# A hybrid attention and DeltaNet block: other cost figures in the planner that sets the engines' orders

## The chip, the cores and the metric

The kernel runs on one core of one Trainium2 chip. The metric is the device time of one execution in microseconds (us); a comparison uses the median over several executions. The core has five engines that work at once, each in the order of its own instruction list: TensorE (PE, with its weight loads PEld), VectorE (DVE), ScalarE (ACT), GpSimd (POOL) and SyncE (SP). DMA transfers are issued from SP, ACT and POOL. An engine whose next instruction waits for a semaphore holds back everything behind that instruction on the same engine.

## The reference, cut to what matters

One layer over 1024 tokens of 1024 channels. The normed input is projected to 7184 columns; two token mixers read them in parallel; gates merge their outputs; an output product, a residual and a final norm follow.

```
h    = rmsnorm(x, norm_w);  proj = h @ w_in
# mixer A: three dilated window attentions (dilation 1, 4, 16), rotary positions, 8 heads of 64
q, k = rope(q), rope(k)
o_g  = softmax(q k^T / 8, masked) v          # for g = 0, 1, 2
o_a  = sum_g softmax_g(lse_g) * o_g
# mixer B: gated DeltaNet, chunks of 64 tokens
q, k, v = silu(conv4(.));  q, k = l2norm(.)
T    = (I + strict(beta k k^T * decay))^-1   # triangular solve, per chunk and head
u, w = T (beta v), T (beta k exp(G))
scan over chunks: v_new = u - w S;  o = q_dec S + attn v_new;  S = S*dec + k_dec^T v_new
# both
y = sig(gate_a) * (o_a*silu(z_a)) @ w_up_a + sig(gate_b) * (rms(o_b)*silu(z_b)) @ w_up_b
out = rmsnorm(x + y @ w_out, final_norm_w)
```

## The kernel before, in words

**Products.** The projection goes in units of 256 columns. Operands are split into a high and a low float16 part, and every product is three matmuls (lines L184, L185, L186: high by high, low by high, high by low), most with a moving block of 512 columns. Some units, the four value blocks among them, go as seven products of sums of blocks (`seven_products`, L355) in place of eight; DVE adds those sums (L329) and ACT and DVE split them (L330). These seven products are the same in the kernel before and after. Weights come through two `wstage` buffers, loaded by POOL (the first ones by SP), and are split by ACT into `whi` (L167) and by DVE into `wlo` (L84 is the line of the helper that issues most DVE operations with three operands, L87 that of the ones with two).

**Stages.** The start (0 to about 45 us) loads x and the first weights, norms, and makes the first queries and keys (L444 to L480). Then come the three attentions, each in two halves of four heads (`att_run`, L758): scores (L790, L792), the masked maximum on DVE (L799, tile `sm`), the exponent on ACT (L803), transposes on PE (L813, into a bank `ps_G`), a split of the transposed weights (`th` on ACT, L818; `tl` on DVE) and the product with the values (L840, `Vh` and `Vl`). `combine` (L866) reads partial results `og` back by DMA and copies their statistics `md` (L873). Projection matmuls of later units are fed in between, so that PE has work while a softmax is under way. From about 440 us on come the DeltaNet's decay terms (L1080 to L1129; `softplus` needs an ACT table of its own, loaded at L1091, and the exponent's table is loaded again at L803), its short convolution (`conv_unit`, L993: tiles `xc` and `ca`), the pairs of keys, and for each half of the heads (`hb` = 0, 1) a triangular solve on DVE (`solve`, L1305: X in 31 pairs of steps, then X times `bsc`, then T1). The solve writes X and T1 to DRAM (`u_d`, `t_d`) and gathers them again with DMAs of 128-byte runs: four pieces into `MT` (L1335) and two pieces into `T1p` (L1333). `merge` (L1339) multiplies them with small matmuls (L1350 left, which reads `T1p`, and L1365 right, which reads `Y`). Then come the chunk states, the scan over chunks, the up-projection, the output product and the final norm.

**What sets the order.** PE's order is written out by hand. The orders of DVE, ACT, POOL and SP are made when the program is built, by a planner at the end of the file. `steps_of` (L2064) turns every instruction into a `Step` with the steps that must end before it (`deps`) or only be issued before it (`turn`). `Step.cost` (L2013) gives each a time for which it holds its engine (`hold`) and a time until its result is there (`ns`), from its shape:

```
kb = w[0].total / 1024
self.hold, self.ns, self.pass_ns = 330 + 0.25 * kb, 2000 + (2.2 if w[0].dram else 5.5) * kb, 60
if min(w[0].piece, r[0].piece) < 256:
    self.hold = 1400 if kb > 64 else 600
    self.ns = self.hold + 2500
if self.eng == "POOL":
    self.hold = 530
```

`fill` (L2132) plays the program through with these figures: whenever an engine is free, it takes of the steps whose inputs are there the one with the lowest rank. `set_orders` (L2196) makes a forward pass by written order, a backward pass that gives each step its latest start, another forward pass by these latest starts, and so on, and keeps the order of the pass that ended first (`PASSES = 2`). The order so found is fixed in the program. Stretches of the program inside `with in_order():` (L496, the start, and L1910, the end) keep their written order on DVE and ACT, DMAs left out.

Of the kernel before, what the change touches and what calls it, by code (L numbers as in the profile page):

```python
# [17 lines left out]
PSUM = bass.MemoryType.PSUM  # L18
# [60 lines left out]
def hybrid_block(ctx: ExitStack, tc: tile.TileContext, A):  # L79
# [415 lines left out]
    ss = base.tile([128, 8], F32, name="ss0")  # L495
    with in_order():  # L496
        wq, wk = w_first
# [1451 lines left out]
TABLE_NS = 1283  # L1949
TILE_SWITCH_NS = 150  # L1950
PASSES = 2


class Operand:


    def __init__(self, b, write):
        size = SIZES[b.dtype]
        ap = [tuple(x) for x in b.ap]
        self.name, self.size, self.write, self.dram = b.tensor.name, size, write, "DRam" in type(b.tensor).__name__  # L1960
        self.psum = b.tensor.name.startswith("ps_")
        if self.dram:
# [29 lines left out]
    def meets(self, o):  # L1992
        if not self.psum and not all(a[0] < b[1] and b[0] < a[1] for a, b in ((self.rows, o.rows), (self.bytes, o.bytes))):
            return False
        return self.dram or self.psum or (self.mask() & o.mask()) != 0


class Step:


    def __init__(self, i, ins):
        self.i, self.ins, self.kind = i, ins, type(ins).__name__
        self.deps, self.turn, self.succ = set(), set(), []
        self.table, self.small, self.hold, self.ns, self.pass_ns = 0, False, 0, 0, 35
        self.args = []
        self.eng = None
        if self.kind not in ("BassTilePoolBoundary", "InstTileManualSchedule"):
            self.eng = ENGINES[str(ins.engine).split(".")[-1]]
            self.args = [Operand(a.bass_ap, w) for l, w in ((ins.outs, True), (ins.ins, False)) for a in l
                         if getattr(a, "bass_ap", None) is not None]  # L2010
            self.cost()

    def cost(self):  # L2013
# [16 lines left out]
        elif self.kind == "InstDMACopy":  # L2030
            kb = w[0].total / 1024
            self.hold, self.ns, self.pass_ns = 330 + 0.25 * kb, 2000 + (2.2 if w[0].dram else 5.5) * kb, 60
            if min(w[0].piece, r[0].piece) < 256:
                self.hold = 1400 if kb > 64 else 600
                self.ns = self.hold + 2500
            if self.eng == "POOL":
                self.hold = 530
        elif self.eng == "DVE":
# [25 lines left out]
def steps_of(tc, in_order):  # L2064
    steps = [Step(i, ins) for i, ins in enumerate(tc.nc.cur_bb.bb.instructions)]
    written, read, users, place = {}, {}, {}, {}
    for s in steps:
        for x in s.args:
            for j, y in written.get(x.name, []) + (read.get(x.name, []) if x.write else []):
                if j not in s.deps and x.meets(y):  # L2070
                    s.deps.add(j)
        for x in s.args:
            (written if x.write else read).setdefault(x.name, []).append((s.i, x))
            users.setdefault(x.name, set()).add(s.i)
        s.deps.discard(s.i)

    def behind(later, earlier):
        for i in later:
            steps[i].deps.update(j for j in earlier if j < i)

# [20 lines left out]
    for s in steps:  # L2101
        if s.kind != "BassTilePoolBoundary" or s.ins.bass_pool_name not in pools:
# [14 lines left out]
    for a, b in in_order:  # L2117
        last = {}
        for s in steps[a:b]:
            if s.eng in ("DVE", "ACT") and s.kind != "InstDMACopy":  # L2120
                if s.eng in last:
                    s.deps.add(last[s.eng])
                last[s.eng] = s.i
    for s in steps:
        s.deps = {j for j in s.deps if steps[j].eng}
        s.turn -= s.deps | {s.i}
        for j in s.deps | s.turn:
# [3 lines left out]

def fill(steps, rank, back):  # L2132
# [4 lines left out]
    free, due, open_ = {e: 0.0 for e in order}, {e: [] for e in order}, {e: [] for e in order}  # L2137
    pe = [s.i for s in steps if s.eng == "PE"][::-1 if back else 1]
    events, blocked, table, small = [(0.0, e) for e in order], set(), 0, None

    def known(i):
        if steps[i].eng not in (None, "PE"):
            heapq.heappush(due[steps[i].eng], (ready[i], i))

    for s in steps:
        if not left[s.i]:
            known(s.i)
    while events:
        t, e = heapq.heappop(events)
        if t < free[e]:  # L2150
            heapq.heappush(events, (free[e], e))
            continue
        if e == "PE":
            if len(order[e]) == len(pe):
                continue
            i = pe[len(order[e])]
            if left[i]:
# [5 lines left out]
        else:  # L2163
# [19 lines left out]
        for j in s.deps | s.turn if back else s.succ:  # L2183
            o = steps[j]
            ready[j] = max(ready[j], t + s.hold + o.until(s) - o.hold if back else t + extra + s.until(o))
            left[j] -= 1
            if not left[j]:
                known(j)
                if o.eng in blocked:
                    blocked.discard(o.eng)  # L2190
                    heapq.heappush(events, (max(free[o.eng], ready[j]), o.eng))
    assert sum(len(x) for x in order.values()) == sum(s.eng is not None for s in steps)
    return start, order, max(t + s.ns for s, t in zip(steps, start))


def set_orders(tc, in_order):  # L2196

    steps = steps_of(tc, in_order)
    rank = [float(s.i) for s in steps]
    best = None  # L2200
    for _ in range(PASSES):
        start, order, end = fill(steps, rank, False)
        if best is None or end < best[0]:
            best = end, order
        late = fill(steps, [-t for t in start], True)[0]
        rank = [-t - s.hold for s, t in zip(steps, late)]
    start, order, end = fill(steps, rank, False)
    if end < best[0]:
        best = end, order
    order_only = mybir.DependencyInfo(mybir.DependencyClass.NoSync, mybir.DependencyReason.DATA)  # L2210
    for e, ids in best[1].items():
# [3 lines left out]
    return best[0]  # L2215

# [105 lines left out]
```

## Time and profile before

| what | value |
|---|---|
| median of 3 executions | 1079.28 us (1072.13 to 1081.35) |
| the profiled execution | 1086.27 us |
| its span, first to last instruction | 1084.5 us |
| TensorE's mean granted clock in it | 0.990 |
| busy DVE in it | 879.6 us (81%) |
| busy ACT in it | 572.0 us (53%) |
| first matmul, and the end of the last | 5.18 us and about 1077 us |

A matmul's record is longer than the time for which it holds PE: matmuls are pipelined, so the pitch from one start to the next counts. A row of the timeline gives the start, the duration, the engine, the line, the operation with its tiles, and in brackets the idle time before it with what ended it. In a window's row the columns are the window's length, the busy time of PE, PEld, DVE, ACT and POOL, then PE's granted clock, the DMA share and GB/s.

### The profile page before, as it was taken

How to read it: one execution, taken by the hardware profiler on the slowest of the kernel's cores; microseconds unless marked ns; L12 is line 12 of the kernel's file. 1: busy time of each engine (PE TensorE's matmuls, PEld its weight loads, DVE VectorE, ACT ScalarE, POOL GpSimd, SP SyncE). 2: the span in 40 equal slices, each digit the busy share in tenths (PEclk: the TensorE clock that was granted, in tenths of full speed). 3: DMA queues.
4: the chain of work that ended last, by engine and by line, in shares of the span. 5: the costliest groups of instructions: out<-in, count | busy, mean ns of one | idle time of the engine just before them, and what ended most of it. 6: DMA issues, size and time to landing. Idle time of an engine off the chain costs nothing.

```text
span 1084.5 us, 24950 instructions
## 1 busy us (share of the span) xinstructions
PE 1047.0 (97%) x9986; PEld 639.9 (59%) x9986; DVE 879.6 (81%) x2030; ACT 572.0 (53%) x1306; POOL 56.1 (5%) x107
## 2 busy tenths in 40 slices
PE   6999999999989999989999999999899999999997
PEld 5995695865846855866655545545445555444444
DVE  6897988979959889989956797796288669799934
ACT  6445766766656666657645623244244336434523
POOL 0000000000000000000010000110200000000000
PEclk9999999999999999999999999999899999999999
DMA  7243532532623622551233466766675413743132
GB/s 259 77 137 97 138 107 85 139 93 84 177 70 103 166 90 75 145 159 45 65 133 106 122 167 185 253 200 207 203 257 175 154 60 129 289 156 117 59 117 78
DMA packets 99780, 148.53 MB, mean 137 GB/s; under 512 B 31168, under 2 KB 64704, under 8 KB 98512
## 3 DMA queue, kind: packets, MB, share of 16 engines
q1 hardware_dynamic: 69264, 84.64, 26.9%
q0 software_dynamic: 12320, 44.11, 12.8%
q10 hardware_dynamic: 18080, 18.20, 4.8%
q8 instruction: 78, 1.28, 0.5%
q14 instruction: 38, 0.31, 0.1%
HBM read 91.13 MB, written 36.90 MB: 118 GB/s over the span
## 4 chain that ended last, share of the span: by engine, by line
PE 41%; DVE 14%; issue 3%; DMA 3%; ACT 3%; POOL 0%; ACTq 0%; DVEq 0%; SPq 0%; POOLq 0%
PE ps_mm L184 10%; PE ps_mm L186 9%; PE ps_mm L185 9%; DVE ca L84 3%; PE ps_S L186 1%; PE ps_S L185 1%; PE ps_S L184 1%; DVE sm L799 1%; DVE tl L87 1%; DVE wlo L84 1%; PE ps_G L186 1%; PE ps_G L185 1%; PE ps_G L184 1%; DMA wn_d<-uw 1%; PE ps_S L1706 1%
## 5 line engine op out<-in xcount | busy, mean ns | idle before, releaser
L186 PE MATMUL ps_mm<-h_hi,wlo 128*128 128x512 f16 (+1 forms) x552 | 208.9, 378 | 0.0
L184 PE MATMUL ps_mm<-h_hi,whi 128*128 128x512 f16 (+1 forms) x492 | 186.6, 379 | 0.0
L185 PE MATMUL ps_mm<-h_lo,whi 128*128 128x512 f16 (+1 forms) x492 | 186.3, 379 | 0.0
L186 PEld LDWEIGHTS <-wlo 128*128 128x128 f16 x788 | 77.4, 98 | 87.2 <-issue 1.8
L185 PEld LDWEIGHTS <-whi 128*128 128x128 f16 x848 | 83.5, 98 | 72.7 <-issue 6.3
L184 PEld LDWEIGHTS <-whi 128*128 128x128 f16 x848 | 83.6, 99 | 69.3 <-issue 1.4
L803 ACT ACTIVATE sm<-sm,osb 128x128 f32<-128x128 f32 (+1 forms) x160 | 69.3, 434 | 63.4 <-DVE osb L799 62.5
L799 DVE CUSTOM_DVE_ANT_0 sm<-ps_S,amask 128x128 f32<-128x128 f32 (+1 forms) x192 | 59.4, 346 | 8.4 <-PE ps_S L792 8.4
L87 DVE TENSOR_TENSOR tl<-ps_G,th 128x256 f16<-128x256 f32 (+1 forms) x96 | 52.0, 542 | 17.3 <-ACT th L818 16.7
L84 DVE SCALAR_TENSOR_TENSOR wlo<-wstage,whi 128x1024 f16<-128x1024 f32 x42 | 51.1, 1220 | 17.5 <-ACT whi L167 15.7
L330 ACT ACTIVATE whi<-wstage 128x512 f16<-128x512 f32 x76 | 46.0, 626 | 32.0 <-DVE wstage L329 9.8
L185 PE MATMUL ps_mm<-wlo,h_hi 128*128 128x256 f16 (+1 forms) x256 | 57.3, 246 | 0.0
L84 DVE SCALAR_TENSOR_TENSOR whi<-wstage,whi 128x512 f16<-128x512 f32 x76 | 51.9, 686 | 6.6 <-ACT whi L330 6.2
L84 DVE SCALAR_TENSOR_TENSOR ca<-xc,cw,ca 128x512 f32<-128x512 f32 x72 | 53.8, 747 | 2.6 <-ACT ca L1010 2.1
L167 ACT ACTIVATE whi<-wstage 128x1024 f16<-128x1024 f32 x41 | 42.7, 1053 | 22.0 <-PE ps_mm L185 11.6
L813 PE MATMUL ps_G<-cons,sm 128*128 128x128 f32 x280 | 48.5, 278 | 5.2 <-ACT sm L803 4.5
L329 DVE TENSOR_TENSOR wstage<-wstage 128x512 f32<-128x512 f32 x76 | 52.1, 688 | 1.1
L813 PEld LDWEIGHTS ps_G<-cons,sm 128*128 128x128 f32 x280 | 35.0, 142 | 21.7 <-ACT sm L803 7.4
L818 ACT CAST th<-ps_G 128x256 f16<-128x256 f32 (+1 forms) x96 | 43.8, 456 | 5.3 <-PE ps_G L813 4.4
L184 PE MATMUL ps_mm<-whi,h_hi 128*128 128x256 f16 (+1 forms) x192 | 46.5, 256 | 0.0
L186 PE MATMUL ps_mm<-whi,h_lo 128*128 128x256 f16 (+1 forms) x192 | 46.2, 255 | 0.0
L184 PE MATMUL ps_mm<-h_hi,wlo 128*128 128x512 f16 x120 | 45.6, 380 | 0.0
(489 smaller groups left out, 2893.6 us busy)
## 6 DMA issues: line engine op xcount, KB each, us to landing
wstage<-in_w POOLq DMA_DIRECT2D x68, 512.0 KB, 4.6
og<-osb ACTq DMA_DIRECT2D x32, 132.0 KB, 2.2
og<-og SPq DMA_DIRECT2D x32, 132.0 KB, 2.3
gspb<-gst ACTq DMA_DIRECT2D x16, 256.0 KB, 4.2
sga<-gspa SPq DMA_DIRECT2D x8, 512.0 KB, 9.6
wstage<-in_w_up POOLq DMA_DIRECT2D x8, 512.0 KB, 4.4
sgb<-gspb SPq DMA_DIRECT2D x8, 512.0 KB, 4.0
wos<-in_w_out SPq DMA_DIRECT2D x8, 512.0 KB, 4.1
```

The costliest lines, as they stand in the source:

```text
L84: (eng or V).scalar_tensor_tensor(out, in0, scalar, in1, op0=op0, op1=op1)
L87: (eng or V).tensor_tensor(out, in0, in1, op)
L167: SC.activation(hi[:, 4 * c:4 * c + 4], st, AF.Copy, scale=W_SCALE)
L184: PE.matmul(out, lhsT=wh(k), rhs=mh(k), start=first and i == 0, stop=False, skip_group_check=True)
L185: PE.matmul(out, lhsT=wh(k), rhs=ml(k), start=False, stop=False, skip_group_check=True)
L186: PE.matmul(out, lhsT=wl(k), rhs=mh(k), start=False, stop=last and i == len(ks) - 1, skip_group_check=True)
L329: V.tensor_tensor(self.part[name], self.part[x], self.part[y], ALU.add)
L330: SC.activation(t[:, b, 0], self.part[name], AF.Copy, scale=W_SCALE)
L799: V.tensor_tensor_reduce(P[:, u, :128 * nk], psc[:, u * 256:u * 256 + 128 * nk], mask, -cexp, -NEG, ALU.add, ALU.min, accum_out=osb[:, 256 ...
L803: SC.activation(P[:, u, :128 * nk], P[:, u, :128 * nk], AF.Exp, bias=osb[:, 256 + hd:257 + hd], scale=-1.0, accum_out=osb[:, 260 + hd:261 ...
L813: PE.transpose(pt[:, c:c + 128], P[:, u, i * 128:i * 128 + 128], ident)
L818: SC.copy(th[:, :n], pt[:, :n])
```

## The change: what it does

The diff touches only the planner and one `in_order`. No instruction is added to the kernel, none is taken away, PE's order is the same row for row (14460 rows), and so is POOL's; what changes is in which order DVE, ACT and SP do the same work. Line numbers after L1950 shift.

- DMAs cost more in the plan: until landing 2800 ns + 4 or 7 ns a KB (before 2000 + 2.2 or 5.5), another 2800 ns where runs are under 256 bytes; issue 350 to 590 ns by the number of rows. A queue moves a KB in 4 ns, and a transfer that is behind others on its queue lands later.
- DVE and ACT operations cost 3% more, a change between small and large matmul tiles 300 ns (before 150). Both kernels make three forward and two backward passes; the constant counted the backward ones and now counts the forward ones.
- `in_order` fixes the order on every engine but PE, DMAs included, as an order of issue; and the first stretch now begins at the program's first instruction, so the first loads go in written order.
- Accesses to one DRAM tensor bind each other only where they meet byte for byte.

```diff
-    def in_order():
-        n = len(nc.cur_bb.bb.instructions)
+    def in_order(first=None):
+        n = len(nc.cur_bb.bb.instructions) if first is None else first
...
-    with in_order():
+    with in_order(0):
...
-TILE_SWITCH_NS = 150
-PASSES = 2
+TILE_SWITCH_NS = 300
+QUEUE_NS = 4
+PASSES = 3
...
-        return self.dram or self.psum or (self.mask() & o.mask()) != 0
+        return self.psum or (self.mask() & o.mask()) != 0
...
-            self.hold, self.ns, self.pass_ns = 330 + 0.25 * kb, 2000 + (2.2 if w[0].dram else 5.5) * kb, 60
+            rows = max(x.rows[1] - x.rows[0] for x in self.args)
+            self.hold = 590 if rows <= 32 else 500 if rows <= 64 else 350
+            self.ns, self.pass_ns, self.kb = 2800 + (4 if w[0].dram else 7) * kb, 60, kb
             if min(w[0].piece, r[0].piece) < 256:
                 self.hold = 1400 if kb > 64 else 600
-                self.ns = self.hold + 2500
+                self.ns += 2800
             if self.eng == "POOL":
-                self.hold = 530
+                self.hold = 530 if rows > 64 else 630
...
+        if self.eng in ("DVE", "ACT") and not self.kb:
+            self.hold, self.ns = 1.03 * self.hold, 1.03 * self.ns
...
-            if s.eng in ("DVE", "ACT") and s.kind != "InstDMACopy":
+            if s.eng not in (None, "PE"):
                 if s.eng in last:
-                    s.deps.add(last[s.eng])
+                    s.turn.add(last[s.eng])
...
-        start[i], free[e] = t, t + s.hold + extra
+        start[i], free[e] = t, t + s.hold + late
+        if s.kb and not back:
+            moved[e] = max(moved[e], t) + s.kb * QUEUE_NS
+            late = max(0, moved[e] + 1200 - t - s.ns)
```

How the rows move is shown at three places. The first is DVE in the attention of the second group, at about 298 us of the profile before; `md_5829` waits for the DMA of `og_5826`, `Vl_3943<-ps_mm_3945` is what frees a bank for PE, and `sm_4518` is the first softmax of the next half. Before:

```order
L84 SCALAR_TENSOR_TENSOR Vl_3943<-rx_4394,Vh_3942 128x4x128
L873 COPY md_5829<-og_5826 128x16
L84 SCALAR_TENSOR_TENSOR Vl_3943<-ps_mm_3945,Vh_3942 128x4x128
L84 SCALAR_TENSOR_TENSOR wlo_4481<-wstage_3966,wlo_4481 128x512
L799 ISA sm_4518,osb_4512<-ps_S_4513,amask_757 128x128
```

After:

```order
L84 SCALAR_TENSOR_TENSOR whi_4449<-wstage_3966,whi_4449 128x512
L84 SCALAR_TENSOR_TENSOR Vl_3943<-ps_mm_3945,Vh_3942 128x4x128
L84 SCALAR_TENSOR_TENSOR wlo_4481<-wstage_3966,wlo_4481 128x512
L873 COPY md_5829<-og_5826 128x16
L799 ISA sm_4518,osb_4512<-ps_S_4513,amask_757 128x128
```

The copy `md` went from ahead of that `Vl` to behind it and behind `wlo`, but stands ahead of `sm` still.

The second place is ACT at the decay terms, at about 477 us; `ba`, `bg` and `tmpa` are the decay terms' tiles, `xc_7352` and `ca_7355` belong to a convolution, `sm_7413` to the softmax for which PE's next transposes wait. Before:

```order
L1080 ACTIVATE ba_7193<-ps_O_7194 128x128
L1094 ACTIVATE ea_7375<-cons_78 128x8
L1085 ACTIVATE bg_7365<-ba_7193 128x64
L1090 ACTIVATE tmpa_7366<-tmpa_7366 128x64
L1091 ACT_TABLE_LOAD
L1091 ACTIVATE tmpa_7366<-tmpa_7366,onec_87 128x64
L1008 COPY xc_7352<-ps_mm_7327 128x512
L900 COPY osb_6503<-ps_G_7396 128x256
L1010 ACTIVATE ca_7355<-ps_mm_7327,cw_84 128x512
L901 DMA oa_d_733<-osb_6503 128x2x128
L803 ACT_TABLE_LOAD
L803 ACTIVATE sm_7413,osbs_7407<-sm_7413,osbs_7407 128x128 x2
```

After:

```order
L1080 ACTIVATE ba_7193<-ps_O_7194 128x128
L1094 ACTIVATE ea_7375<-cons_78 128x8
L1008 COPY xc_7352<-ps_mm_7327 128x512
L1010 ACTIVATE ca_7355<-ps_mm_7327,cw_84 128x512
L1085 ACTIVATE bg_7365<-ba_7193 128x64
L900 COPY osb_6503<-ps_G_7396 128x256
L1090 ACTIVATE tmpa_7366<-tmpa_7366 128x64
L901 DMA oa_d_733<-osb_6503 128x2x128
L1091 ACT_TABLE_LOAD
L1091 ACTIVATE tmpa_7366<-tmpa_7366,onec_87 128x64
L803 ACT_TABLE_LOAD
L803 ACTIVATE sm_7413,osbs_7407<-sm_7413,osbs_7407 128x128 x2
```

The two copies and `ca` went from between the two table loads to ahead of the first. On DVE, `ba` moved ahead of both `wlo` pieces there, and `sm_7413` ahead of eight rows of the decay terms.

The third place is SP behind the second solve (`hb` = 1), at about 721 us. Before:

```order
L1326 DMA u_d1_9510<-X_9411 128x1024
L1327 DMA t_d1_9511<-T1_9508 128x1024
L1335 DMA MT1_8544<-u_d1_9510 32x32x32
L1333 DMA T1p_9514<-t_d1_9511 32x32x32 x2
L1335 DMA MT1_8544<-u_d1_9510 32x32x32 x2
L1393 DMA kbt_10633<-kb_d1_8558 128x1024
L1335 DMA MT1_8544<-u_d1_9510 32x32x32
L1393 DMA kbt_10637<-kb_d1_8558 128x1024
```

After:

```order
L1326 DMA u_d1_9510<-X_9411 128x1024
L1327 DMA t_d1_9511<-T1_9508 128x1024
L1335 DMA MT1_8544<-u_d1_9510 32x32x32 x4
L1333 DMA T1p_9514<-t_d1_9511 32x32x32 x2
L1393 DMA kbt_10633<-kb_d1_8558 128x1024
L1393 DMA kbt_10637<-kb_d1_8558 128x1024
```

Both `T1p` pieces went behind all four `MT` pieces, and both `kbt` behind all six. On DVE, one `wlo` piece and one `ca` now stand ahead of X times `bsc` of this solve, and one more `ca` ahead of `T1_9508`. At the start, SP now issues `cons`, `amask` and the two key-weight pieces ahead of the fourth x tile and of the `xs` tiles, which stood ahead of them.

More of the change, by code (lines that the diff above doesn't have):

```diff
@@ L2077, in behind @@
     def behind(later, earlier):
-        for i in later:
-            steps[i].deps.update(j for j in earlier if j < i)
+        if later and earlier:
+            steps.append(Step(len(steps), None))
+            steps[-1].deps |= earlier
+            for i in later:
+                steps[i].deps.add(steps[-1].i)
     for t in tc.info.tiles:
@@ L2100, in steps_of @@
                 used[n] |= users.get(t.name, set())
-    for s in steps:
+    for s in list(steps):
         if s.kind != "BassTilePoolBoundary" or s.ins.bass_pool_name not in pools:
@@ L2136, in fill, with passed @@
     start, order = [0.0] * len(steps), {e: [] for e in ENGINES.values()}
-    free, due, open_ = {e: 0.0 for e in order}, {e: [] for e in order}, {e: [] for e in order}
-    pe = [s.i for s in steps if s.eng == "PE"][::-1 if back else 1]
-    events, blocked, table, small = [(0.0, e) for e in order], set(), 0, None
+    free, moved, due, open_ = [{e: x() for e in order} for x in (float, float, list, list)]
+    events, blocked, table, small, end = [(0.0, e) for e in order], set(), 0, None, 0.0
     def known(i):
[L2142 to L2147, printed above, removed]
+        e = steps[i].eng
+        if e is None:
+            passed(steps[i], ready[i], 0)
+        elif e not in given:
+            heapq.heappush(due[e], (ready[i], i))
+        if e in blocked:
+            blocked.discard(e)
+            heapq.heappush(events, (max(free[e], ready[i]), e))
+    def passed(s, t, late):
+        for j in s.deps | s.turn if back else s.succ:
+            o = steps[j]
+            if back:
+                ready[j] = max(ready[j], t + s.hold + o.until(s) - o.hold)
+            else:
+                ready[j] = max(ready[j], t + late * (s.i in o.deps) + s.until(o))
+            left[j] -= 1
+            if not left[j]:
+                known(j)
+    for i in [s.i for s in steps if not left[s.i]]:
+        known(i)
     while events:
@@ L2179, in fill, with orders_of @@
             small = s.small
-        start[i], free[e] = t, t + s.hold + extra
+        start[i], free[e] = t, t + s.hold + late
+        if s.kb and not back:
+            moved[e] = max(moved[e], t) + s.kb * QUEUE_NS
+            late = max(0, moved[e] + 1200 - t - s.ns)
+        end = max(end, t + late + s.ns)
         order[e].append(i)
         heapq.heappush(events, (free[e], e))
[L2183 to L2191, printed above, removed]
-    assert sum(len(x) for x in order.values()) == sum(s.eng is not None for s in steps)
-    return start, order, max(t + s.ns for s, t in zip(steps, start))
+        passed(s, t, late)
+    assert sum(len(x) for x in order.values()) == sum(s.eng is not None for s in steps)
+    return start, order, end
+def orders_of(steps):
+    given = {"PE": [s.i for s in steps if s.eng == "PE"]}
+    rank, best = [float(s.i) for s in steps], None
+    for n in range(PASSES):
+        start, order, end = fill(steps, rank, False, given)
+        if best is None or end < best[0]:
+            best = end, order
+        if n < PASSES - 1:
+            late = fill(steps, [-t for t in start], True, given)[0]
+            rank = [-t - s.hold for s, t in zip(steps, late)]
+    return best[1]
 def set_orders(tc, in_order):
     steps = steps_of(tc, in_order)
[L2199 to L2209, printed above, removed]
     order_only = mybir.DependencyInfo(mybir.DependencyClass.NoSync, mybir.DependencyReason.DATA)
-    for e, ids in best[1].items():
+    for e, ids in orders_of(steps).items():
         if e != "PE":
```

44 lines of the change are left out of this document (29 added, 15 removed).

## The prediction, before the change was run

> **What bounds the kernel now.** First the page's table of busy time, then the waits of PE.
>
> ```profile
> PE 1047.0 (97%) x9986; PEld 639.9 (59%) x9986; DVE 879.6 (81%) x2030; ACT 572.0 (53%) x1306; POOL 56.1 (5%) x107
> ```
>
> PE is busy for 1047.0 of the span's 1084.5 us. Its instructions and their order do not change, so the change can win only what PE waits, 37.5 us at most with the start and the end, and what a lowered clock costs. Whom PE waits for:
>
> ```profile
> PE ps_mm L502 <- DVE nwd L87: 5.2, 1, 5.2
> PE ps_G L813 <- ACT sm L803: 4.5, 3, 3.5
> PE ps_S L1266 <- ACT uw L1424: 3.9, 1, 3.9
> PE ps_mm L184 <- DVE Vl L84: 3.5, 1, 3.5
> PE ps_O L840 <- DVE tl L87: 1.8, 4, 0.6
> PE ps_O L1247 <- DVE rq L1251: 1.4, 1, 1.4
> PE ps_mm L184 <- ACT gst L948: 1.0, 1, 1.0
> PE ps_G L1266 <- ACT qT L1021: 1.0, 1, 1.0
> PE ps_G L1365 <- DVE Y L87: 0.7, 2, 0.5
> ```
>
> The columns are the total, the number of waits and the longest. The list is short, and three waits of 3.5 to 3.9 us stand out. What they cost beyond themselves is in the windows of 25 us (PE's granted clock is the third column from the end):
>
> ```profile
> 300.00:325.00 25.00, 21.47 (x136) 11.80 (x135) 14.65 (x44) 13.30 (x40) 0.53 (x1) 0.93 0.18 64
> 475.00:500.00 25.00, 21.53 (x117) 11.29 (x114) 19.51 (x72) 15.56 (x43) 1.05 (x2) 0.86 0.27 74
> 750.00:775.00 25.00, 20.57 (x438) 12.51 (x437) 6.95 (x11) 5.76 (x10) 5.61 (x9) 0.87 0.46 135
> 775.00:800.00 25.00, 23.55 (x217) 12.12 (x216) 15.53 (x31) 11.47 (x21) 1.92 (x4) 0.99 0.77 259
> ```
>
> A clock of 0.93 over 25 us is a shortfall of 1.75 us, 0.86 one of 3.5. Only windows with a wait of 3.5 us or more show one; the wait of 1.4 us (at 789) does not. So a long wait costs 5.3 to 7.4 us, and shortening it below the point where the clock falls is worth more than its length.
>
> **The change part by part.** It gives DVE, ACT and SP another order. For each wait I compare the two orders ahead of the instruction waited for, with durations from rows.
>
> *At 300 us.* DVE stands at a copy of statistics until a DMA lands, and the `Vl` that frees PE's bank is behind it:
>
> ```profile
> 303.29 0.17 DVE L873 COPY md<-og 128x16 f32<-128x16 f32 x1 [5.06 <-DMA og<-og]
> 303.38 0.68 DVE L84 SCALAR_TENSOR_TENSOR Vl<-ps_mm,Vh 128x512 f16<-128x512 f32 x1
> 304.57 0.28 DVE L799 CUSTOM_DVE_ANT_0 sm<-ps_S,amask 128x128 f32<-128x128 f32 x1
> 304.90 0.40 ACT L803 ACTIVATE sm<-sm,osb 128x128 f32<-128x128 f32 x1 [3.94 <-DVE osb L799]
> 304.11 0.38 PE L184 MATMUL ps_mm<-sum1h,whi 128*128 128x512 f16 x1 [3.53 <-DVE Vl L84]
> 307.95 0.38 PE L813 MATMUL ps_G<-cons,sm 128*128 128x128 f32 x2
> ```
>
> Now `Vl` and `wlo` run in DVE's idle 5.06 us, and PE goes on at 304.11 - 3.53 = 300.6. From 304.11 to its transposes at 307.95 it has 3.84 us of work, done at half the clock; at the full clock that is 2.0, so PE gets there at 302.6. What is late next is `sm`, still behind `md`: 303.38 instead of 304.57, so its exponent ends at 304.1 and PE's transposes start near 304.5. A wait of 1.9 replaces 3.53, and the shortfall of 1.75 goes: 3.53 + 1.75 - 1.9 gives **-3.4** (0 if the new wait still lowers the clock and the landing is later, -5.3 if nothing waits).
>
> *At 482 us.* The path is ACT's, with two table loads:
>
> ```profile
> 477.42 0.28 ACT L1080 ACTIVATE ba<-ps_O 128x128 f32<-128x128 f32 x1 [4.40 <-DMA og<-og]
> 480.98 0.26 ACT L1090 ACTIVATE tmpa<-tmpa 128x64 f32<-128x64 f32 x1 [1.35 <-DVE tmpa L84]
> 481.25 1.28 ACT L1091 ACT_TABLE_LOAD   x1
> 482.55 0.35 ACT L1091 ACTIVATE tmpa<-tmpa,onec 128x64 f32<-128x64 f32 x1
> 484.25 1.28 ACT L803 ACT_TABLE_LOAD   x1
> 485.54 0.40 ACT L803 ACTIVATE sm<-sm,osbs 128x128 f32<-128x128 f32 x1
> 486.09 0.86 PE L813 MATMUL ps_G<-cons,sm 128*128 128x128 f32 x2 [3.47 <-ACT sm L803]
> ```
>
> Between 482.90 and 484.25 ACT does `xc`, a copy and `ca`, 1.35 us; these go ahead, into its idle time. On DVE `tmpa` no longer waits behind both `wlo`, about 0.5 us earlier, and `sm` stands ahead of the decay terms. The exponent then starts 1.35 + 0.5 = 1.9 earlier. PE's wait becomes 1.6 and the shortfall of 3.5 goes: **-5.4** (-1.4 if the clock falls all the same, -7.0 if both go).
>
> The rows leave open where between 1.4 and 3.47 us the clock starts to fall; if 1.9 and 1.6 were enough, the two terms would shrink by 1.75 and 3.5, and the time be 1077. [...]
>
> *The start.* The second weight piece for the keys arrives late, and `h_hi` and `h_lo` stand behind its split:
>
> ```profile
> 20.61 1.06 ACT L167 ACTIVATE whi<-wstage 128x1024 f16<-128x1024 f32 x1 [3.33 <-DMA wstage<-in_w]
> 22.20 0.61 PE L478 MATMUL ps_mm<-h_hi,whi 128*128 128x128 f16 x8 [0.67 <-ACT h_hi L469]
> 23.58 0.61 PE L478 MATMUL ps_mm<-h_lo,whi 128*128 128x128 f16 x8 [0.77 <-DVE h_lo L84]
> ```
>
> SP now issues it ahead of 2.5 MB of x; 0.67 + 0.77 go, and one small row ahead of the first matmul costs 0.15: **-1.3**. What takes its place behind the waiting SP row is the fourth x tile; +2 if that is late.
>
> *Smaller ones.* Two more rows of DVE:
>
> ```profile
> 611.23 0.69 DVE L1237 TENSOR_REDUCE kss<-ps_S 128x8 f32<-128x512 f32 x1 [2.94 <-ACT ps_S L1236]
> 787.96 0.69 DVE L84 SCALAR_TENSOR_TENSOR whi<-wstage,whi 128x512 f16<-128x512 f32 x1 [3.08 <-ACT whi L330]
> ```
>
> In front of the `tl` of four waits stand 0.6 to 3 us less DVE work: **-1.2** (0 to -1.8). At 788, DVE's `rq` moved ahead of the split `whi`, which came only after 3.08 us of idling for a weight, and ACT's part of the sums moved likewise: **-1.4** (0 to -1.4). The gate's `gst` at 399 has two ACT rows more ahead of it: **+0.8** (0 to +1.2). At 608 to 628 the first solve's rows moved ahead of the sums `kss` on DVE, 2.6 us of work against the 2.94 us that DVE idles there; what is not hidden falls on PE: **+0.7** (0 to +3). `qT` at 726: **+0.3** (0 to +0.5). The `uw` wait at 766 has the same rows ahead of it on DVE, ACT and POOL: 0.
>
> *The second solve, at 721 us.* This speaks against the change:
>
> ```profile
> 722.25 1.22 DVE L84 SCALAR_TENSOR_TENSOR wlo<-wstage,whi 128x1024 f16<-128x1024 f32 x1
> 724.05 1.22 DVE L84 SCALAR_TENSOR_TENSOR wlo<-wstage,whi 128x1024 f16<-128x1024 f32 x1
> 724.06 0.32 SPq L1335 DMA_DIRECT2D MT<-u_d  x1
> 728.94 4.96 SPq L1335 DMA_DIRECT2D MT<-u_d  x2
> 734.55 0.44 SPq L1335 DMA_DIRECT2D MT<-u_d  x1
> DMA to landing us min/median/max: 2.8/6.2/7.9
> 739.75 1.20 PE L1350 MATMUL ps_S<-T1p,MT 32*32 32x32 f32 x64
> ```
>
> The first of these `wlo` and one `ca` between the two now come before X is done: X is 724.05 - 722.25 = 1.8 us later, T1 another `ca` later, which its transfer, second in the queue, can bear. The six pieces take 16.7 us from the first issue to the landing of the last (734.55 + 6.2 - 724.06; the landing row is that of L1335), 0.6 of it a `kbt` that now goes behind. `T1p`, needed first, now lands last: 724.06 + 1.8 + 16.1 = 742.0, and PE comes at 739.75. The wait of 2.3 hides the 0.7 of `Y`: **+1.6** (-0.7 if it fits; at most +11: five pieces at 2.5 us, then the longest landing of `T1p`, 9.0, is 747.3, 7.6 late, and a shortfall of 3.5).
>
> ```profile
> DMA to landing us min/median/max: 3.5/5.4/9.0
> ```
>
> [...]
>
> *What I do not see.* Some 2600 lines of DVE's order differ; new short waits will arise. The waits of at most 0.8 us in the whole list sum to some 4 us; half of it: **+2.0** (0 to +4).
>
> *Sum.* -3.4 - 5.4 - 1.3 - 1.2 - 1.4 = -12.7; +0.8 + 0.7 + 0.3 + 1.6 + 2.0 = +5.4: -7.3. The profiled execution of 1086.27 us becomes 1079.0. It lies 7.0 above the median of the runs, 1079.28; against that the time is **1072.0 us**.
>
> **The rivals.** *The waits move and do not go* (transfers set the ends): at 300 `sm` stays behind `og`, and PE stops at the transposes for as long; at 482 two loads stay. Then -1.3 - 0.6 - 0 - 1.4 - 1.4 + 5.4 is +0.7: 1080 us. For it speaks that `md` is ahead of `sm` in both orders; against it the 5.06 us of idle DVE. *All goes well*: every listed gain at its bound, -16.9, `T1p` in time, -0.7, no unseen loss, +0.8: -16.8, 1062.5 us. For it speaks that a planner with later landings moves waiting rows back everywhere, not only where I looked. *T1p comes last and late*: the +11 above instead of +1.6, -7.3 + 9.4 = +2.1: 1081.4 us, slower than before. It decides from a landing behind 743.2 on, where the wait passes 3.47 us and the clock falls too. For it speak the 9.0 of the landing row and a queue that is used for weights as well.
>
> **How the numbers follow.** Chances: the forecast 0.45, moved waits 0.23, all well 0.20, late `T1p` 0.12. The forecast's own terms give some 6 us to either side, 1066 to 1078; the range reaches to the others, 1060 to 1085. About 1% (10.8 us) is what a measurement of this kernel can tell from no change. Faster than 1068.5: all of the well-going case and 0.3 of the forecast, 0.34. Slower than 1090: late `T1p` together with moved waits and unseen losses, 0.09. Within 1%: 0.57.
>
> **What would show it.** Right: no wait of over 2.5 us on PE at 300 and 482, granted clock 1.00 in those windows; L813 still waits for `sm` at 304; no wait for `rq`; a wait of L1350 for `T1p` near 740; the `uw` wait unchanged with 0.87 in its window. Wrong: waits of 3.5 us at places that the list of before doesn't have, or a first softmax behind `og` that waits longer than before.

## The result and the profile after

The kernel after takes 1068.68 us (median of 14 executions, 1063.39 to 1074.1); beside it the kernel before took 1079.39 us (14 executions, 1072.13 to 1091.37). The ratio is 0.990 with a 95% interval of 0.9873 to 0.9927: 10.7 us less. The forecast was 1072.0, with a range of 1060 to 1085. The profiled execution of after took 1070.89 us, 2.2 above the median, with a span of 1069.1; that of before had lain 7 above its median. So the two profiles differ by 15.4 us, some 5 more than the kernels do, and a good part of this study is about those 5.

First the table of busy time and PE's waits in the profile of after, with the columns as before:

```profile
PE 1042.0 (97%) x9986; PEld 639.1 (60%) x9986; DVE 877.7 (82%) x2030; ACT 573.0 (54%) x1306; POOL 56.3 (5%) x107
```

```profile
PE ps_mm L502 <- DVE nwd L87: 5.2, 1, 5.2
PE ps_S L1350 <- DMA T1p<-t_d: 3.6, 2, 2.9
PE ps_S L1266 <- ACT uw L1424: 3.5, 1, 3.5
PE ps_G L813 <- ACT sm L803: 2.0, 2, 1.4
PE ps_mm L184 <- ACT gst L948: 1.5, 1, 1.5
PE ps_O L840 <- DVE tl L87: 1.3, 2, 0.9
```

The wait for `Vl` (3.5 us) and the one for `rq` (1.4) are gone, the one for `sm` at 482 us went from 3.47 to 1.4, and a wait for `T1p`, which before did not have, has now the largest total behind the start. The windows show where the clock still falls:

```profile
300.00:325.00 25.00, 25.00 (x183) 14.34 (x182) 21.70 (x50) 15.96 (x46) 1.06 (x2) 1.00 0.17 55
475.00:500.00 25.00, 25.00 (x202) 15.51 (x201) 24.57 (x89) 19.12 (x58) 0.53 (x1) 1.00 0.19 61
725.00:750.00 25.00, 24.29 (x568) 14.74 (x572) 11.71 (x18) 8.04 (x15) 2.56 (x4) 0.87 0.43 151
750.00:775.00 25.00, 21.48 (x237) 11.77 (x227) 7.93 (x12) 7.38 (x14) 4.69 (x8) 0.86 0.62 206
```

At 300 and 475 us it is 1.00 now; around `T1p` and `uw` it is 0.87 and 0.86. At 300 us, in DVE's timeline:

```profile
294.26 0.69 DVE L84 SCALAR_TENSOR_TENSOR Vl<-ps_mm,Vh 128x512 f16<-128x512 f32 x1
294.87 0.68 DVE L84 SCALAR_TENSOR_TENSOR wlo<-wstage,wlo 128x512 f16<-128x512 f32 x1
295.89 0.17 DVE L873 COPY md<-og 128x16 f32<-128x16 f32 x1 [0.34 <-DMA og<-og]
```

`Vl` runs ahead of `md` as its new place says; but `md` too waits only 0.34 us and not 5.06. The transfer of `og` landed 2.3 us after its issue here (293.58 to 295.9) and 4.9 us after it before (298.41 to 303.29). At 472 us, in ACT's timeline and PE's:

```profile
470.51 1.28 ACT L1091 ACT_TABLE_LOAD   x1
472.17 1.28 ACT L803 ACT_TABLE_LOAD   x1
473.47 0.40 ACT L803 ACTIVATE sm<-sm,osbs 128x128 f32<-128x128 f32 x1
474.01 0.71 PE L813 MATMUL ps_G<-cons,sm 128*128 128x128 f32 x2 [1.36 <-ACT sm L803]
```

The table loads stand back to back, as read from the order. And the second solve, with `X` on DVE, a weight load on POOL, the pieces on SP, and PE:

```profile
702.89 1.22 DVE L84 SCALAR_TENSOR_TENSOR wlo<-wstage,whi 128x1024 f16<-128x1024 f32 x1
704.40 0.56 POOL L313 DMA_DIRECT2D wstage<-in_w  x1 [6.22 <-DVE X L87]
704.80 1.22 DVE L87 TENSOR_TENSOR X<-X,bsc 128x1024 f32<-128x1024 f32 x1
706.08 0.33 SPq L1326 DMA_DIRECT2D u_d<-X  x1
711.59 5.15 SPq L1335 DMA_DIRECT2D MT<-u_d  x4
716.79 3.88 SPq L1333 DMA_DIRECT2D T1p<-t_d  x2
724.94 0.31 PE L1350 MATMUL ps_S<-T1p,MT 32*32 32x32 f32 x2 [2.89 <-DMA T1p<-t_d]
725.96 1.91 PE L1350 MATMUL ps_S<-T1p,MT 32*32 32x32 f32 x62 [0.71 <-DMA T1p<-t_d]
```

Both causes that the prediction named are there, `wlo` ahead of `X` times `bsc` and `T1p` behind four `MT` pieces, and one that it did not name: from the issue of `u_d` to that of the first `MT` piece, which waits for it, pass 5.5 us (706.08 to 711.59) against 2.8 before (721.29 to 724.06). The rows of before:

```profile
721.29 0.33 SPq L1326 DMA_DIRECT2D u_d<-X  x1
723.77 0.56 POOL L313 DMA_DIRECT2D wstage<-in_w  x1 [8.07 <-DVE wlo L84]
```

In both profiles POOL's 512-KB weight load goes out 0.3 us behind the end of the first `wlo`, for which it waits by the row of before. Since that `wlo` now runs ahead of `X`, the load goes out 1.7 us ahead of `u_d`, where before it went out 2.5 us behind it. By the records of the packets, POOL's queue moved 472 KB and ACT's 452 KB while `u_d` was under way in after, and neither moved any in before.

**A table by stage.** PE does the same 9986 matmuls in the same order in both kernels. So the time between the same two matmuls can be compared in any two profiles, whatever was shifted ahead of them. The stages here are bounded by the matmuls that ran at the given times in the first profile of before; the numbers are worked out from the starts of these matmuls. The last row is the rest of the span; in it the profiles differ by up to 3.5 us, mostly at 245 to 298, 320 to 395 and 500 to 540 us. e1 to e5 are experiments below; e1 is the kernel before and e5 the kernel after, each profiled once more.

| stage (us of before) | before | e1 (before) | e2 | e3 | after | e5 (after) | e4 |
|---|---|---|---|---|---|---|---|
| 0 to 50, start | 50.0 | 49.7 | 50.6 | 49.6 | 48.3 | 48.1 | 47.6 |
| 215 to 245, K pieces | 30.2 | 32.7 | 33.1 | 28.8 | 28.3 | 27.9 | 27.5 |
| 298 to 320, `md`, `Vl` | 22.2 | 17.1 | 19.0 | 20.7 | 16.8 | 16.8 | 16.8 |
| 475 to 500, decay, `sm` | 24.9 | 22.4 | 20.2 | 19.5 | 20.1 | 19.7 | 21.5 |
| 540 to 560 | 20.1 | 20.1 | 20.6 | 20.6 | 18.7 | 18.8 | 18.7 |
| 700 to 735, `qT` | 35.1 | 34.6 | 34.8 | 35.4 | 33.7 | 33.7 | 35.3 |
| 735 to 743, `T1p` | 7.9 | 7.9 | 7.9 | 7.9 | 14.5 | 13.1 | 8.6 |
| 743 to 756, `Y` | 13.0 | 13.0 | 13.0 | 13.0 | 11.7 | 11.7 | 13.8 |
| 764 to 785, `uw` | 21.0 | 18.2 | 21.2 | 20.4 | 20.5 | 18.0 | 17.8 |
| 785 to 800, `rq` | 15.0 | 17.5 | 14.6 | 14.9 | 13.3 | 13.3 | 13.3 |
| behind the last matmul | 7.6 | 7.6 | 7.6 | 7.6 | 6.9 | 6.9 | 6.9 |
| all other stages together | 837.6 | 837.3 | 839.4 | 839.7 | 836.4 | 838.1 | 836.2 |

### The profile page after: what moved, and what is told of

It is laid out like the page before. It is cut to its first block, busy times and chain, and to the rows that moved or that the text cites. A ratio compares the mean times of both kernels' runs of the same rounds, so it can differ in the third digit from the quotient of the medians.

```text
span 1069.1 us, 24944 instructions
## 1 busy us (share of the span) xinstructions
PE 1042.0 (97%) x9986; PEld 639.1 (60%) x9986; DVE 877.7 (82%) x2030; ACT 573.0 (54%) x1306; POOL 56.3 (5%) x107
## 3 DMA queue, kind: packets, MB, share of 16 engines
q0 software_dynamic: 12320, 44.11, 13.1%
## 4 chain that ended last, share of the span: by engine, by line
PE 67%; DVE 14%; DMA 7%; issue 5%; ACT 4%; SPq 2%; ACTq 0%; DVEq 0%; POOLq 0%
PE ps_mm L184 16%; PE ps_mm L185 16%; PE ps_mm L186 16%; DMA wstage<-in_w 2%; PE ps_S L185 2%; PE ps_S L184 2%; PE ps_S L186 2%; DVE tl L87 1%; SPq L629 1%; DVE ca L84 1%; PE ps_G L813 1%; ACT sm L803 1%; DVE sm L799 1%; DVE wlo L84 1%; PE ps_G L184 1%
## 5 line engine op out<-in xcount | busy, mean ns | idle before, releaser
L87 DVE TENSOR_TENSOR tl<-ps_G,th 128x256 f16<-128x256 f32 (+1 forms) x96 | 52.0, 542 | 15.4 <-ACT th L818 14.8
L185 PE MATMUL ps_mm<-h_lo,wlo 128*128 128x512 f16 x120 | 45.5, 379 | 0.0
```

Of the source, the lines that this page charges most:

```text
L87: (eng or V).tensor_tensor(out, in0, in1, op)
L185: PE.matmul(out, lhsT=wh(k), rhs=ml(k), start=False, stop=False, skip_group_check=True)
```

## The experiments

Theory: the rows that stand ahead of an instruction on its engine set PE's long waits, so that each move of rows brings what its place says. First rival: the long waits of the profile of before were in part chance, transfers that landed late in that execution, and moving rows wins less. Second rival, on where the gain is from: the longer transfer figures, as against the first loads or the rest.

In e2, e3 and e4 a small function behind the planner moves single steps in an engine's finished order; everything else stays. `at` finds a step by its engine, the tile that it writes and one that it reads, and `move` puts it in front of (with `True`: behind) another.

### e1: the kernel before, again

No edit.

> The kernel before, unchanged, profiled once more. If the order of the rows sets the long waits, PE waits about 3.5 us at 300 us (for Vl), 482 us (for sm) and 766 us (for uw) again, and the span is within 3 us of 1084.5. If the wait at 300 us was a late landing of og by chance of that execution (the profiled one lay 7 us above the median of its runs), it is shorter by 2 us or more here, its window's clock is 1.00, and the span is nearer to 1077.

Measured: 1079.89 us in this one execution, a span of 1078.1. PE's waits and the windows of this profile:

```profile
PE ps_G L813 <- ACT sm L803: 2.6, 2, 2.0
PE ps_S L790 <- issue: 2.6, 1, 2.6
PE ps_O L1247 <- DVE rq L1251: 2.3, 1, 2.3
PE ps_S L1266 <- ACT uw L1424: 2.2, 2, 1.9
PE ps_mm L184 <- DVE Vl L84: 0.2, 1, 0.2
```

```profile
300.00:325.00 25.00, 24.83 (x173) 14.00 (x172) 17.91 (x52) 15.92 (x48) 0.75 (x2) 1.00 0.25 77
475.00:500.00 25.00, 22.91 (x160) 12.98 (x159) 23.03 (x91) 18.91 (x52) 0.88 (x2) 0.93 0.21 65
775.00:800.00 25.00, 22.75 (x215) 11.11 (x214) 17.13 (x37) 10.75 (x20) 1.37 (x3) 0.93 0.76 247
```

The rival is right about this profile: with the same rows, the wait for `Vl` is 0.2 us in place of 3.5, the one for `sm` 2.0 in place of 3.5, while the one for `rq` is longer. The stage at 298 to 320 us takes 17.1 and not 22.2. A wait's length in one profile is a sample, not the kernel's.

### e2: before, with `md` behind `Vl` and `wlo`

```diff
+    md = at("DVE", "md_5829", "og_5826")
+    move("DVE", md, at("DVE", "sm_4518"))
```

> The kernel before with one move on DVE: the copy md goes behind Vl and wlo at 300 us. If rows behind md held PE, no wait for Vl is left there, a wait for sm of 0 to 1.9 us takes its place, and the time falls by 3.4 to 5.4 us against an execution that has the wait of 3.5 (ratio about 0.996). If the wait only moves to the transposes, PE waits there for over 3 us and the ratio is 1.000. If the wait was chance, nothing is left to win in most executions: ratio 0.999 to 1.000.

Measured: ratio 0.9998 (0.9958 to 1.0039). No wait for `Vl` is left in its profile; one for `sm` of 1.7 us came, and ended at 307 us, with a clock of 1.00 in the window:

```profile
PE ps_G L813 <- ACT sm L803: 3.8, 3, 1.7
```

So the row does what its place says (`md` late, `sm` next, 1.7 us; the prediction had 1.9), but the executions show no gain: the stage takes 19.0 here against 22.2, 17.1 and 20.7 in the three profiles with the old rows, 20.0 on average, and the interval of 4 us to either side can't resolve 1 us. At 475 to 500 us, where e2 has the rows of before, PE waited 1.5 us and the stage took 20.2: the third sample of a wait that was 3.5 and 2.0.

### e3: before, with the moves at 482 us

```diff
+    for w, r in (("xc_7352", "ps_mm_7327"), ("osb_6503", "ps_G_7396"), ("ca_7355", "ps_mm_7327")):
+        move("ACT", at("ACT", w, r), at("ACT", "bg_7365"))
+    m = at("DVE", "xc_7352")
+    move("DVE", at("DVE", "ba_7193"), m)
+    move("DVE", at("DVE", "bg_7365", "ba_7193"), m + 1)
+    move("DVE", at("DVE", "tmpa_7366", "bg_7365"), at("DVE", "wlo_7386", "wstage_7325"))
+    sm = at("DVE", "sm_7413")
+    for k in range(2):
+        move("DVE", sm + k, at("DVE", "bg_7365", "tmpa_7366"))
```

> The kernel before with the moves at 482 us alone: on ACT xc, the copy and ca go ahead of the decay terms, on DVE ba, bg and tmpa ahead of wlo, and sm ahead of the decay terms' rows. Forecast: the exponent starts 1.9 us earlier, PE waits about 1.6 us, the clock of the window is 1.00: 5.4 us less, ratio 0.995. Rival, the two table loads keep the wait above 3 us or 1.6 us is enough for the clock to fall: 0 to 1.9 us less, ratio 0.998 to 1.000.

Measured: ratio 1.0015 (0.9979 to 1.0051). In its profile the longest wait for `sm` is 0.6 us and the stage takes 19.5, the shortest of the four; but `Vl`, at the untouched 300 us, waits 2.0 us, and the clock falls for it:

```profile
PE ps_mm L184 <- DVE Vl L84: 2.0, 1, 2.0
PE ps_G L813 <- ACT sm L803: 1.3, 3, 0.6
```

```profile
300.00:325.00 25.00, 24.04 (x158) 13.48 (x158) 17.80 (x51) 14.65 (x45) 0.53 (x1) 0.93 0.12 41
```

The wait at its place went, the 5.4 us did not come: the stage gave 5.4 against the first profile (24.9 to 19.5), but 3.0 against the mean of the three with the old rows (22.5), and the executions exclude more than 2.3 us. At 500 to 540 us both e2 and e3 took 1.2 to 1.5 us more than before; whether the moves did that stays open, since e2's moves are far from there.

### e4: after, with `T1p` behind one `MT` piece

```diff
+    for n in (0, 1):
+        move("SP", at("SP", "T1p_9514", n=n), at("SP", "MT1_8544", "u_d1_9510") + n, True)
```

> The kernel after with the two T1p pieces issued behind the first MT piece, as before, and not behind all four. If the order on SP makes the wait for T1p (2.9 + 0.7 us at 722 us and a clock of 0.87 over 25 us, 3.4 us more), the wait is under 1 us, the clock 1.00, and the time falls by 4 to 6 us against the kernel after (ratio to before about 0.985). If X and T1, which DVE makes later now, and the late landing of u_d make it, 2 us or more of the wait stay, and the gain is 0 to 2 us (ratio 0.988 to 0.990).

Measured: 1066.78 us (1065.3 to 1069.06), ratio to before 0.990 (0.9867 to 0.9933). The wait for `T1p` is gone; these are in its list now, and the clock is full in both windows:

```profile
PE ps_G L813 <- ACT sm L803: 3.4, 2, 2.8
PE ps_S L1266 <- ACT uw L1424: 3.4, 1, 3.4
PE ps_G L1365 <- DVE Y L87: 1.6, 3, 0.7
```

```profile
725.00:750.00 25.00, 23.38 (x538) 14.03 (x531) 14.57 (x22) 11.11 (x21) 3.63 (x6) 1.00 0.52 174
750.00:775.00 25.00, 21.62 (x226) 11.68 (x224) 11.40 (x22) 9.33 (x18) 3.92 (x8) 1.00 0.78 246
```

The order on SP made the wait: stage 735 to 743 falls from 14.5 and 13.1 to 8.6, although `X` is as late as in after. Of these 4.5 to 5.9 us, 2.1 come back as waits for `Y` (743 to 756: 11.7 to 13.8). The median is 1.9 us under after's 1068.68, less than the 4 to 6 expected, and the ratio to before is after's 0.990 with an interval of over 3 us to either side: it is the stage that shows the wait to go, not the time.

At 475 to 500 us e4 has the rows of after, and yet PE waited 2.8 us for `sm` and the stage took 21.5. On DVE a copy `md` that waits for `og` stands ahead of the decay terms there, in after's order too:

```profile
468.35 0.17 DVE L873 COPY md<-og 128x16 f32<-128x16 f32 x1 [1.51 <-DMA og<-og]
```

### e5: the kernel after, again

No edit.

> The kernel after, unchanged, once more: a second profile of the same orders. If the change took away waits that came and went from execution to execution, the stages at 215 to 245, 298 to 320, 475 to 500 and 785 to 800 us (PE's times of before) are again within 1.5 us of the first profile of after, 28.3, 16.8, 20.1 and 13.3 us, while the kernels before spread over 3 to 5 us there; the wait for T1p is again 2 to 4 us. If the first profile of after was a lucky one, one of these stages is 2 us or more longer.

Measured: 1069.22 us (1067.79 to 1070.54), ratio 0.9906 (0.9875 to 0.9937). All four stages are within 0.5 us of the first profile. The wait for `T1p` is 2.6 and 0.6 us, the clock falls for half as long, and the wait for `uw` is 1.9 us in place of 3.5:

```profile
PE ps_S L1350 <- DMA T1p<-t_d: 3.2, 2, 2.6
PE ps_S L1266 <- ACT uw L1424: 2.2, 2, 1.9
```

```profile
725.00:750.00 25.00, 24.07 (x582) 14.60 (x583) 12.22 (x19) 8.23 (x16) 2.55 (x4) 0.93 0.45 157
```

Over 215 to 245, 298 to 320, 475 to 500 and 785 to 800 us the two profiles of before take 92.3 and 89.7 us together, those of after 78.5 and 77.7. At 298 to 320 us the wait that came and went is gone: after, e4, e5 and e7 to e9, which all have the same rows there, take 16.8 us. At 475 to 500 us it is not gone for good, as e4 shows. This joins theory and rival: the order of the rows decides whether PE waits, and how much a new order wins depends on how late the transfers land.

### e6: after, with the old transfer figures

```diff
-            rows = max(x.rows[1] - x.rows[0] for x in self.args)
-            self.hold = 590 if rows <= 32 else 500 if rows <= 64 else 350
-            self.ns, self.pass_ns, self.kb = 2800 + (4 if w[0].dram else 7) * kb, 60, kb
+            self.hold, self.ns, self.pass_ns = 330 + 0.25 * kb, 2000 + (2.2 if w[0].dram else 5.5) * kb, 60
+            self.kb = kb
...
-QUEUE_NS = 4
+QUEUE_NS = 0
```

The figures for short runs and for POOL go back as well.

> The kernel after with the DMA costs of before in the planner (issue, landing, short runs, POOL) and no queue time; everything else as after. In its orders md is ahead of Vl again at 300 us and T1p behind two MT pieces. If the longer transfer figures make most of the gain, as the change's words have it, the ratio to before is 0.995 to 1.000. If the loads at the start, the dependencies and the other figures make it, the ratio is 0.988 to 0.992.

Measured: 1071.64 us, ratio 0.9919 (0.9888 to 0.9949): 2.4 us over e5 in the same comparison, with intervals that overlap. So most of the gain stays without the longer transfer figures; the second side of the expectation holds. Its profile has the waits of before again where those figures had moved rows:

```profile
PE ps_S L790 <- DMA Ks<-pcl: 1.9, 1, 1.9
PE ps_O L1247 <- DVE rq L1251: 1.9, 2, 1.3
PE ps_mm L184 <- DVE Vl L84: 1.0, 1, 1.0
```

The stage of the K pieces takes 30.5 (after 28.3 and 27.9), that at 298 to 320 us 18.0, that at 785 to 800 us 14.9.

### e7: after, with the first loads free

```diff
-    with in_order(0):
+    with in_order():
```

> The kernel after with in_order from where it stood before, so the first loads are ordered by the planner again: wk goes behind the x tiles. The prediction's term of the start says 1.3 us, the first comparison of profiles 1.7: the first 50 us of PE take 49.7 to 50.1 us again, the rest is as after, ratio to before 0.9915. If the start's gain is eaten later in after, the ratio is 0.990 as with it.

Measured: 1072.45 us, ratio 0.9935 (0.9911 to 0.9958), 3.2 us over e5; the executions overlap a little (1069.26 to 1075.58 against 1067.79 to 1070.54). PE's first 50 us take 49.6, 1.4 more than the mean of after and e5; the wait for `T1p` and the stage of `uw` were also among the long ones in its profile (13.8 and 20.1). The start is worth the 1.3 that the prediction gave it, or somewhat more.

### e8: after, with 150 ns for a change of tile size

```diff
-TILE_SWITCH_NS = 300
+TILE_SWITCH_NS = 150
```

> The kernel after with the old 150 ns for a change between small and large matmul tiles. In its orders T1p stands behind one MT piece as before the change, the other places at 300 and 482 us and the start are as after. If the order on SP made the wait for T1p, stage 735 to 743 us is 8 to 8.6 us in place of 14.5, 743 to 756 gets 1.3 to 2.1 longer, and the time is 4 us under after's: ratio to before 0.986. If other rows that moved eat that, 0.989 to 0.991.

Measured: 1065.74 us (1062.44 to 1067.71), ratio 0.9869 (0.9839 to 0.99): 3.5 us under e5. Stage 735 to 743 takes 7.9, 743 to 756 takes 12.5. All six executions lie below all six of e5. With this one figure back, `T1p` stands behind one `MT` piece again, so the figure had put it last. It moves more than that, though: DVE and ACT have other rows from 469 us on, and `X` times `bsc` is ahead of `wlo` again, and `u_d` landed 2.6 us after its issue and not 5.5. What the place of `T1p` alone does is in e4.

### e9 to e11: the slot of `uw`, and no 3%

The longest single wait left after e8, behind the start, is the one for `uw`. Four `uw` tiles share three buffers, and the last copy on ACT waits until the two `un_d` transfers that POOL issued out of its buffer have landed (the second at 756.07 us in after, where the copy starts at 756.21). e9 is e8 with this edit; the buffer of `T1p` is dead by then:

```diff
-                    uw = p2_.tile([128, 4, 2, 64], F32, name="uw", tag="rv", bufs=3)
+                    if hb and g and x and r:
+                        uw = p2_.tile([128, 8, 4, 32], F32, name="uw4", tag="T1p", bufs=1)
+                        uw = uw.rearrange("p a b c -> p (a b c)")[:, 0:512].rearrange("p (t q i) -> p t q i", q=2, i=64)
+                    else:
+                        uw = p2_.tile([128, 4, 2, 64], F32, name="uw", tag="rv", bufs=3)
```

> The kernel of e8 in which the last uw copy of the second half on ACT gets the space of T1p, dead by then, instead of a fourth turn in the three rv buffers. If that copy waits for its slot, that is for the un_d transfers that POOL issues in a row, PE's wait for uw (2.3 to 4.0 us at 754 to 766 us, at 3.5 and more with a lowered clock) falls under 1.5 us, stage 764 to 785 us is 15.5 to 16.5 us, and the time is 1 to 3 us under e8's: ratio to before about 0.985. If the other uw copies' slots hold PE as long, the stage stays at 16.7 to 18 and the ratio at 0.987.

Measured: 1061.22 us (1059.85 to 1065.78), ratio 0.9824 (0.979 to 0.9858), an interval that lies below after's as well. No wait for `uw` is in its list, and stage 764 to 785 takes 14.3 us, less than expected. The first rows of that list behind the start, and a window:

```profile
PE ps_G L813 <- ACT sm L803: 2.6, 2, 2.0
PE ps_mm L184 <- ACT gst L948: 1.5, 1, 1.5
```

```profile
475.00:500.00 25.00, 25.00 (x196) 15.20 (x195) 23.59 (x89) 18.48 (x54) 0.00 (x1) 0.95 0.16 49
```

e10 is the kernel after, and e11 the kernel after with the edit of e9, both with `pass` in place of the line that multiplies `hold` and `ns` by 1.03.

> The kernel after without the 3% on DVE and ACT operations. In its orders T1p stands behind one MT piece, X times bsc comes ahead of wlo and ca, and at 482 us ACT makes the first four exponents before the first table load. By the order of the rows: stage 735 to 743 us is 7.9 to 8.6 us in place of 14.5, and the wait for sm at 482 us is under 0.5 us (stage 475 to 500: 18.3 to 18.8): 5 to 6 us under after, ratio to before 0.985. If waits that the 3% had avoided appear elsewhere, the ratio is 0.988 to 0.991.

> The kernel of e10 with the uw slot of e9. If both reasons hold and add up: 1 to 3 us under e10, ratio to before about 0.983. If one of them eats the other: as e10.

Measured: e10 1070.0 us, ratio 0.9898 (0.9865 to 0.9931); e11 1064.24 us, ratio 0.9843 (0.9808 to 0.9877). In e10 both places came out nearly as expected, stage 735 to 743 at 7.9 and 475 to 500 at 19.6 (18.3 to 18.8 expected), with no wait for `sm` over 0.6 us, and the time is after's all the same: it lost 1.1 us at 50 to 215, 1.1 at 298 to 320 and 2.1 at 395 to 410 us (the wait for `gst` is 2.0). The expectation was too high by what other rows lost. e11 won 5.8 on e10, more than the 1 to 3 expected: stage 764 to 785 takes 14.1 against 19.7, and the wait for `uw`, 3.8 us in e10's profile, is not in its list. But at 478 us, where e10 and e11 have the same rows, e11's PE waited 3.1 us for `osb`, a wait that e10's profile does not have, and stage 475 to 500 took 24.4.

## Why the prediction was right, and where not

The direction, the size and the range held: 1072.0 forecast, 1068.7 measured. Its terms did less well than their sum.

*The sum against one execution.* The prediction set its terms against the profiled execution and carried the difference to the median. Some of its terms were waits that this execution had longer than others: the one at 300 us (3.53, then 0.2 in e1 and 2.0 in e3) and the one at 482 us (3.47, 2.0 and 1.5). In the two profiles these gave 5.4 and 4.9 us, near the predicted 3.4 and 5.4. Against the means of the profiles of the old rows, 20.0 and 22.5, the two profiles of after win 3.2 and 2.6. The step at 300 us has its size by this, though on another path (next paragraph); that at 482 us was twice too large, and e2 and e3, which make these moves alone, won nothing that the executions show. That the sum came out 3.3 us from the measured time is in part luck: the term at 482 us promised some 3 us too much and the one of `T1p` some 3 too little cost, and gains that the prediction had not named made up for both.

*At 300 us,* the prediction had `sm` waiting 1.9 us behind the late `og`. In after `og` was not late and nothing waited; e2 has the predicted case, with 1.7. The step that was missing is what makes `og` late. SP's issue of `og` and POOL's next weight load stand close together, here in before (two rows) and in after (two rows):

```profile
297.93 0.53 POOL L313 DMA_DIRECT2D wstage<-in_w  x1 [19.36 <-DVE whi L84]
298.41 1.55 SPq L870 DMA_DIRECT2D og<-og  x3
293.58 1.56 SPq L870 DMA_DIRECT2D og<-og  x3
294.29 0.53 POOL L313 DMA_DIRECT2D wstage<-in_w  x1 [19.41 <-ACT Vh L749]
```

By the records of the packets, in before, e2, e3, e10 and e11 POOL's queue moved 490 to 870 KB while the first of these `og` was under way, and it landed 3.7 to 5.2 us after its issue; in the other eight profiles the queue moved at most 64 KB in that time, and `og` landed in 2.3 to 2.6 us. With the rows of before the load goes out between 0.5 us ahead of `og` and 0.5 us behind it, so that both cases occur; with those of after it goes out 0.4 to 1.5 us behind. No experiment moves the load alone.

*The start:* -1.3 predicted, -1.6 between the means of the two profiles each of before and after, +1.4 in e7 when undone. Right.

*`T1p`:* +1.6 predicted, +5.3 measured in after (735 to 756: 20.9 to 26.2) and +3.8 in e5. The place and the order on SP were right (e4 undoes it); the size was off. The term took the wait as 2.3 us with a full clock. It was 2.9 and 0.7, with `u_d` 2.7 us longer under way, and the clock fell, for 6.8 us at half rate in after. The prediction counted what the `wlo` ahead of `X` costs DVE, and not that the weight load behind this `wlo` then runs beside `u_d`: `u_d` landed in 5.3 to 5.8 us in all four profiles with that row order (after, e4, e5, e7) and in 2.6 to 2.8 in before, e1 to e3, e8 and e9, where the other queues moved at most 112 KB beside it. In e6, e10 and e11 `X` is ahead of `wlo`, but other transfers of 476 to 833 KB ran beside `u_d`, and it took 4.1 to 5.5. The rival of the late `T1p` had priced this with up to 11, from a wait beyond 3.47 on: the clock fell already at 2.9 (0.87) and, in e5, at 2.6 (0.93). The four `MT` pieces landed 5.2 to 7.0 us after their issue in after, the two of `T1p` 6.4 to 8.1.

*`rq`:* -1.4 predicted, -1.7 measured; in e1 it was worth 4.2. `tl`: -1.2 predicted; PE's waits for it sum to 1.8 us in before and e1, 1.3 in after and 1.8 in e5, so little came of it. `gst`: +0.8 predicted, +0.5 measured. The rows at 608 us: +0.7 predicted, 0 measured; DVE's idle time covered them (3.5 us ahead of `kss` in before, none in after).

*What I do not see:* +2.0 predicted, and this was the wrong sign. Waits that the prediction had not named went: 215 to 245 us, 1.9 us (2.3 for e5; the K pieces are issued in fours from both tiles alternately and no longer six of one first); 540 to 560, 1.3; 700 to 735, 1.4, where it had +0.3; the end, 0.7. The argument, half of the small waits come as new ones, had no mechanism behind it. The rival of the well-going case had the reason for such gains, rows that move back everywhere and not only at the places looked at (its own sum, -16.9, is -16.8).

*`uw`:* the same rows, as predicted; its stage took 20.5 and 18.0 us in the two profiles of after, 21.0 and 18.2 in those of before: it differs as much between equal kernels as between the two.

*The point where the clock falls* was left open between 1.4 and 3.47 us, and the sum counted waits of 1.6 to 2.3 us as if they left it full. That was the author's estimate: none of the rows that the prediction gives has a wait of PE of such a length. In the runs a wait of 1.7 us stood in a window of 1.00 (e2), one of 2.0 in a window of 0.93 (e3); by luck neither of the two shortened waits lowered the clock in after (at 482 us it was 1.4 us there, and 2.8 in e4).

What stays open: which part of the change makes the rest of the gain. Without the transfer figures 2.4 us are lost, without the first loads 3.2, both with intervals that overlap after's, and the tile figure costs 3.5; each moves rows at many places, so these need not add up. The dependencies (`turn`, the DRAM ranges) were not tried alone.

## What to carry to other kernels

Take a second profile of the unchanged kernel before sizing a wait from the first: where an engine waits for a transfer, its length is a sample, and here the samples of one wait ran from 0.2 to 3.5 us. Then ask what else moved while the late transfer was under way, and which row let that start: both late transfers here, `og` and `u_d`, ran beside a weight load of 512 KB. Where PE's order is fixed, compare profiles by the time between the same matmuls; that shows each stage's gain and loss at once. And read a new order from the consumer's side: pieces that a consumer needs first belong first on the queue, whatever a planner's total says.

## What the runs showed of the hardware

In before and after the granted clock has two values between 12 us and the last matmul, 1.00 and 0.50. It was at half five times, each time from late in one of PE's long waits on or from just behind it:

| profile | PE's wait, us | its end, us | clock at 0.50 from, us | for, us |
|---|---|---|---|---|
| before | `Vl`, 3.53 | 304.11 | 304.4 | 3.4 |
| before | `sm`, 3.47 | 486.09 | 485.3 | 6.8 |
| before | `uw`, 3.95 | 769.82 | 768.6 | 6.8 |
| after | `T1p`, 2.89 | 724.94 | 724.8 | 6.8 |
| after | `uw`, 3.52 | 756.85 | 755.5 | 6.8 |

For the experiments the windows of 25 us tell it, where 0.93 is a shortfall of 1.75 us and 0.86 one of 3.5. Waits of 2.0 us (`Vl` in e3), 2.6 (`T1p` in e5) and 3.8 (`uw` in e10) stood in windows of 0.93, one of 2.0 (`sm` in e9) beside windows of 0.98 and 0.95, one of 3.1 (`osb` in e11) in one of 0.86; waits of 1.7 (`sm` in e2), 2.1 (`uw` in e8) and 3.4 (`uw` in e4) stood in windows of 1.00. So the length of a wait alone did not decide it, and what else did is not shown here. This is one reason why equal kernels differ by some microseconds from execution to execution: in these profiles a wait of 2 to 3.5 us cost nothing more (e4), 1.75 us more (e3) or 3.4 (`uw` in after, 6.8 us at half the clock).
